# Partial results set aside in SBUF: their 46 additions move from VectorE to GpSimd, and loads are issued between them

## The chip, the core and the metric

One NeuronCore of a Trainium2 chip runs the kernel. The metric is device time in microseconds of one execution; a smaller number is better. The engines are named as the profile names them: PE (TensorE, matmuls), PEld (its weight loads), DVE (VectorE), ACT (ScalarE), POOL (GpSimd) and SP (SyncE, here only a DMA queue). SBUF is the core's working memory, PSUM the banks in which PE accumulates. POOL has two tasks here: it issues the loads (it writes their descriptors) and it can compute on SBUF.

## The reference

```python
# input: (16, 512, 1024) f32, grad_output: (16, 512, 768) f32
grad_weight = np.einsum('bmk,bmn->kn', input, grad_output)   # (1024, 768) f32
```

Batch and m together are 8192 rows. Every element of the result is a sum over all of them, so the result (3 MB) stays on the core while 58.7 MB of input stream past it.

## The kernel before

**Tiling.** The 8192 rows are cut into 32 units of 256 rows; each unit is one load of X (512 KB as bf16) and one of G (384 KB), converted from f32 to bf16 by the DMA on the way in. The result is cut into quarters A, B, C, D (halves of k by halves of n), and each quarter into four row tiles q = 0..3 of 128 x 384. Six units ("s" in LOADS, the first five and the last) are multiplied directly. The other 26 ("P") hold two rows on each partition, so that X and G are 2 x 2 block matrices; these are multiplied with seven block products in place of eight. The products are called A, B, C (which go to the quarters of that name), 1, 5, 6 and 7. The extra operands of products 5, 6 and 7, and the changed ones of B and C, are sums of blocks: three instructions on X (`sum_x`, lines 206, 208, 210) and three on G (`sum_g`, lines 216, 218, 220) for each unit, all on DVE, bf16, with both operands and the result in SBUF. Below they are called **block sums**: 26 x 6 = 156 instructions.

**Sums in SBUF.** `acc` holds the quarters and `macc` the products 1, 5, 6, 7, all f32. There are eight PSUM banks and 32 sums (8 products x 4 tiles), so a sum gets a bank for a few matmuls and is then closed.

**The order** is written out by hand in PLAN, a string of tokens, and each engine executes its own tokens in just that order. Four engines follow the plan: nothing is reordered.

- `B1@4.2`: open tile 1 of product B in bank 4 and do 2 matmuls; `A0.2` goes on in an open bank (`multiply`, matmul on line 328).
- `f`: ACT copies a sum from SBUF into a bank, so that matmuls add to it (`fill`, line 302).
- `c`, `v`: close a bank: ACT copies it to the sum (line 367), or DVE adds it to the sum (line 371; 369 and 364 are its copy and its last step).
- `z...`: the bank is copied to one of 24 slots `aside` (`set_aside`, line 383), so that it comes free at once, and `y...` later adds the slot to the sum (`add_aside`, line 392, DVE, 46 times, f32 128 x 384, both operands in SBUF). 43 of the copies are ACT's, three are DVE's.
- `x`, `g`: a block sum. `w`: merges two sums on POOL near the end (`merge`, line 399, five times).

**Who waits for an addition.** The next writer of that slot, and the next `f`, `c` or `v` of the same sum. Slots are few in use at first (`aside` 0 to 2) and many later.

**Loads.** All are issued on POOL's queue (lines 175 and 176 for units 2 to 31), G before X, in a loop that stands ahead of the plan; nothing stands between them on POOL. Ten pairs of load buffers are held (`PAIRS_HELD`). A load waits until its buffer is free, and, since there are eight semaphores for such loads, until the load eight places before it has landed.

Of the kernel before, what the change touches and what calls it, by code (L numbers as in the profile page):

```python
# [9 lines left out]
P = 128  # L10

LOADS = "sssssPPPPPPPPPPPPPPPPPPPPPPPPPPs"
# [17 lines left out]
    "zcC2.0 D2@6.2 fD3@3 C3@7.2 yC2.0 D0@4.2 zcD2.1 vC3 D3.2 D1@6.2 vD0 cD3 C1@7.2 yD2.1 A3.4 fB3@3 vD1 "  # L30
    "A2.4 vC1 D3@4.2 A1.4 zcD3.0 B1@6.2 yD3.0 B3.2 vB1 C2@4.2 cB3 D0@7.2 vC2 D2@6.2 zcD0.1 C3@3.2 vD2 "
    "fD1@4 C0.2 B0@7.2 zvC3.0 C1@6.2 yD0.1 zcB0.2 B2@3.4 vC1 D1.4 yC3.0 vB2 D0@7.2 cD1 C3@6.2 yB0.2 "
    "zcD0.1 A0.2 g0.5 A0.2 fC2@4 D3@7.2 zvC3.0 C2.2 g1.5 zcD3.2 B1@6.2 yD0.1 cC2 D2@3.2 zvB1.3 B3@7.2 "
    "zcD2.1 B0@4.1 g2.5 B0.1 zcB3.4 C1@6.1 x0.5 C1.2 zcB0.5 A2.3 yC3.0 zcC1.6 10@3.1 x1.5 12@7.1 A1.3 c10 "
    "yD3.2 c12 C2@4.1 x2.5 C3@6.1 C0.1 zcC2.0 g0.6 C0.2 zcC3.2 11@3.1 yB1.3 13@7.1 A3.2 c11 g1.6 A3.1 c13 "
    "50@4.1 yD2.1 51@6.1 52@3.1 c50 A0.1 g2.6 53@7.1 x0.6 c51 A0.1 70@4.1 C0.1 c52 A1.1 v53 71@6.2 c70 "
    "72@3.1 x1.6 72.1 c71 73@7.2 yB3.4 c72 60@4.2 x2.6 61@6.2 c73 g0.7 62@3.2 c60 63@7.2 v61 c62 A2.1 "
    "g1.7 B0@4.2 c63 yC1.6 B2@3.2 zcB0.3 B1@6.1 g2.7 B1.1 A3.1 zcB2.1 yB0.5 13@4.2 zcB1.4 11@7.1 x0.7 "
    "11.1 A2.1 zc13.6 A0.1 v11 C0.1 C1@3.2 x1.7 10@6.2 zcC1.5 yC2.0 B3@4.2 zc10.7 53@7.1 g0.8 53.1 A3.1 "
    "A1.1 zc53.0 x2.7 70@3.2 vB3 51@6.2 zc70.8 C2@7.1 g1.8 C2.1 zc51.9 yC3.2 12@4.2 C3@3.1 zcC2.10 g2.8 "  # L40
    "C3.1 A1.1 x0.8 A0.1 zcC3.2 50@7.2 52@6.3 v12 zc50.11 71@3.1 x1.8 71.1 zc52.12 A2.1 yB0.3 72@4.2 "
    "zc71.13 73@7.1 g0.9 73.1 zc72.3 A3.1 x2.8 61@6.2 zc73.14 g1.9 63@3.2 v61 C0.1 60@4.2 zc63.15 g2.9 "
    "B2@7.2 y13.6 zc60.16 B1@6.2 zcB2.17 10@3.1 x0.9 10.1 A3.1 f62@4 C0.1 vB1 A2.1 zc10.6 50@7.2 x1.9 "
    "62.2 zc50.18 yB2.1 C2@3.2 c62 51@6.1 x2.9 51.1 A1.1 fB0@7 g0.10 A0.1 B3@4.3 vC2 B0.2 zcB3.1 g1.10 "
    "B0.1 12@3.2 v51 cB0 11@4.1 g2.10 11.1 zc12.19 13@6.3 yB1.4 zc11.20 C3@7.1 x0.10 C3.2 C1@3.3 v13 "
    "53@4.1 x1.10 53.2 zcC1.4 70@6.3 vC3 zc53.21 x2.10 52@3.2 zc70.22 g0.11 71@7.2 zc52.23 61@4.2 yC1.5 "
    "A2.1 f62@6 A0.1 g1.11 B2@3.2 v71 62.2 zcB2.5 C0.1 g2.11 A1.1 c62 x0.11 A1.1 A3.2 f73@3 72@7.2 v61 "
    "f60@6 A2.1 73.1 x1.11 73.2 f12@4 v72 60.3 c73 x2.11 12.2 c60 g0.12 63@7.3 c12 y53.0 B1@3.3 f10@6 "
# [3 lines left out]
    "71.3 c70 y10.7 72@4.2 c71 x2.13 72.1 61@7.1 g0.14 f62@3 61.2 A1.1 v72 fB2@6 A2.1 62.2 g1.14 f10@4 "  # L52
    "62.1 v61 B2.3 c62 g2.14 10.2 f11@7 x0.14 10.1 A3.2 cB2 12@3.3 v10 f73@6 x1.14 11.3 v12 73.2 c11 "
    "x2.14 73.1 60@4.1 f63@3 g0.15 60.2 C0.1 c73 y70.8 A0.1 63.2 fB0@7 g1.15 63.1 B1@6.3 v60 c63 B0.1 "
    "g2.15 fC1@4 B0.2 vB1 A1.2 fC2@3 x0.15 A2.2 f13@6 C1.3 vB0 C2.2 cC1 x1.15 C2.1 13.3 y51.9 f50@7 C0.1 "
    "g0.16 cC2 51@4.3 c13 x2.15 50.2 g1.16 f52@3 50.1 v51 53@6.3 c50 g2.16 52.3 fC3@4 v53 A0.2 fB3@7 "
    "x0.16 C3.3 c52 yC2.10 B3.3 f72@6 x1.16 cC3 70@3.3 vB3 72.2 f62@4 g0.17 72.1 f71@7 A3.2 x2.16 62.2 "
    "c72 g1.17 62.1 71.3 v70 fB2@6 C0.1 c62 g2.17 B2.3 v71 f11@4 61@3.1 x0.17 61.2 f12@7 11.3 cB2 v61 "
    "12.2 c11 x1.17 12.1 73@6.3 yC3.2 c12 10@3.1 x2.17 10.2 f60@7 g0.18 63@4.3 v73 60.3 g1.18 fB1@6 A1.2 "
    "v10 A2.2 c60 g2.18 B1.3 v63 A0.2 x0.18 cB1 C0.2 f50@4 C1@3.3 y52.12 A3.1 x1.18 A3.1 50.3 vC1 B0@7.1 "  # L60
    "x2.18 B0.2 c50 g0.19 13@6.3 fC2@3 vB0 A1.1 f53@4 A2.1 C2.1 g1.19 C2.2 v13 53.3 cC2 g2.19 51@7.1 "
    "x0.19 f52@6 51.2 A0.1 c53 A2.1 v51 52.3 f70@3 x1.19 52.1 fC3@4 61@7.3 y50.11 c52 C3.1 g0.20 C3.2 "
    "f72@6 70.1 x2.19 70.2 cC3 g1.20 72.3 v61 c70 C0.1 g2.20 B3@4.4 c72 y71.13 fB2@7 A1.2 y72.3 f71@6 "
    "A3.2 x0.20 B2.3 vB3 12@3.3 cB2 x1.20 71.4 v12 62@7.1 g0.21 62.3 c71 x2.20 f63@3 60@4.2 g1.21 60.1 "
    "f10@6 A0.1 v62 63.3 g2.21 f11@7 10.4 v60 c63 x0.21 11.4 fC1@4 v10 fB1@3 C0.2 c11 A2.1 x1.21 A2.1 "
    "C1.3 y63.15 f73@6 fB0@7 B1.1 x2.21 B1.2 g0.22 cC1 73.4 cB1 y60.16 B0.1 f13@4 g1.22 B0.3 v73 C2@3.2 "
    "cB0 g2.22 C2.1 13.1 x0.22 f51@6 13.3 f53@7 vC2 A1.2 c13 51.1 x1.22 51.3 f50@3 y73.14 53.2 c51 x2.22 "
    "53.2 g0.23 50.4 c53 yB2.17 A0.2 f52@7 g1.23 A3.2 c50 y10.6 70@6.2 g2.23 70.1 f72@3 C3@4.4 y50.18 "
    "x0.23 A2.2 C0.2 v70 72.3 x1.23 f61@6 72.1 52.3 vC3 c72 x2.23 52.1 61.2 g0.24 c52 61.2 y12.19 B3@4.3 "
    "c61 g1.24 B3.1 f12@7 B2@3.4 y11.20 f62@6 g2.24 12.1 x0.24 12.3 62.3 vB2 c12 A1.2 vB3 c62 60@7.2 "  # L70
    "x1.24 f71@3 60.1 A0.1 g0.25 A0.1 fB1@4 A3.2 x2.24 f63@6 71.2 g1.25 71.2 v60 B1.2 c71 g2.25 B1.2 "
    "yB3.1 63.3 f11@3 x0.25 63.1 cB1 C1@7.4 c63 y53.21 11.2 f10@4 x1.25 11.2 f73@6 vC1 10.3 c11 x2.25 "
    "10.1 fC2@7 73.1 g0.26 73.3 c10 yC1.4 C2.2 fB0@3 g1.26 C2.2 c73 y70.22 13@4.3 cC2 g2.26 B0.4 y52.23 "
    "f50@6 x0.26 f53@7 A2.3 cB0 50.4 v13 f51@3 x1.26 53.4 f70@4 v50 51.1 g0.27 51.3 f61@6 x2.26 c53 70.2 "
    "g1.27 70.2 c51 yB2.5 B3@7.2 c70 g2.27 B3.1 61.3 y11.0 f52@3 C0.1 fC3@4 x0.27 C0.3 c61 A1.3 vB3 x1.27 "
    "A0.3 fB2@7 x2.27 C3.2 g0.28 C3.2 52.2 cC3 g1.28 52.2 72@6.1 g2.28 72.3 c52 A3.3 v72 B2.2 x0.28 f62@6 "
    "B2.2 12@4.2 cB2 x1.28 12.2 60@3.1 f71@7 x2.28 60.4 v12 62.1 g0.29 62.4 fB1@4 v60 B1.2 c62 g1.29 B1.2 "
    "f11@3 g2.29 71.4 vB1 63@6.2 c71 x0.29 63.2 11.4 v63 A2.1 x1.29 fC1@6 A2.2 v11 C2@4.3 g0.30 f13@3 "
    "C2.1 10@7.1 x2.29 10.3 vC2 C1.2 g1.30 C1.2 f11@4 v10 13.3 cC1 g2.30 13.1 A1.1 x0.30 A1.2 c13 12@6.2 "
    "f13@3 11.1 x1.30 10@7.1 A0.3 c11 v12 13.1 x2.30 f61@4 C0.3 v10 f62@6 61.4 v13 f60@7 62.2 f63@3 v61 "  # L80
    "60.2 A3.3 v62 f71@4 63.2 v60 f72@6 71.2 v63 f70@7 A0.2 A1.2 v71 f73@3 A2.3 f51@4 wC1 A3.2 73.5 vA3 "
    "vA0 72.3 v73 51.4 vA1 f53@3 wC3 70.4 vA2 53.4 v72 f52@0 v70 fC1@1 C0.2 52.3 v51 fC2@2 f50@6 C1.3 wB1 "
    "fC3@7 vC0 C2.3 fD1@4 v52 C3.5 cC1 wB2 fD2@5 50.4 v53 fB1@1 fD3@0 D2.2 wB3 B1.4 vC2 cC3 fB2@3 v50 "
    "D1.2 cB1 D3.2 B2.5 fD0@2 vD2 fB0@7 vD3 D0.2 fB3@1+6 vB2 B0.7 vD0 vD1 B3.6 vB0 cB3 "
# [8 lines left out]
MERGED = 2  # L93
# [16 lines left out]
def kernel(  # L110
# [6 lines left out]
    nc = tc.nc  # L117
    bf16 = mybir.dt.bfloat16
    f32 = mybir.dt.float32

    B, M, K = input.shape
# [45 lines left out]
    items = []  # L167
    tiles = {}
    for u, kind in enumerate(LOADS):
        pool = pairs if u else head  # L170
        xp = pool.tile([P, 2, K], bf16, name="xp", tag="xp")
        gp = pool.tile([P, 2, N], bf16, name="gp", tag="gp")
        if u >= MERGED:
            rows = slice(2 * u * P, 2 * (u + 1) * P)
            nc.gpsimd.dma_start(out=gp, in_=G[rows, :].rearrange("(p m) n -> p m n", m=2))  # L175
            nc.gpsimd.dma_start(out=xp, in_=X[rows, :].rearrange("(p m) k -> p m k", m=2))  # L176
        for h in range(2):
            s = 2 * u + h
            if s > 0 and u < MERGED:
                nc.gpsimd.dma_start(out=gp[:, h, :], in_=G[s * P : (s + 1) * P, :])  # L180
            if s > 1 and u < MERGED:
                nc.gpsimd.dma_start(out=xp[:, h, :], in_=X[s * P : (s + 1) * P, :])  # L182
            if kind == "s":
                items.append(("s", xp[:, h, :], gp[:, h, :]))
        tiles[u] = (xp, gp)
        if kind == "P":
            items.append(("P", u, None))

# [35 lines left out]
    x0, x1, g0 = items[0][1], items[1][1], items[0][2]  # L226
# [20 lines left out]
    def operands(p, i, q):  # L247
        kind, x, g = items[i]
        k = slice(q * P, (q + 1) * P)
        if kind == "s":  # L250
            half = slice(KH, K) if p in "CD" else slice(0, KH)
            return x[:, half][:, k], g[:, LEFT if p in "AC" else RIGHT]
        u = x
# [134 lines left out]
    def add_aside(p, q, i):  # L388
        laid.remove((p, q, i))
        assert (p, q) not in opened or not opened[p, q][1]  # L390
        dst = sum_of(p, q)
        nc.vector.tensor_add(out=dst, in0=dst, in1=aside[i])  # L392
# [64 lines left out]
```

## Time and profile before

| | |
|---|---|
| device time, median of 3 runs | 162.1 us (162.03 to 162.11) |
| the profiled execution: span, first to last instruction | 160.0 us |
| left outside the span, median less span | 2.1 us |
| PE busy | 155.1 us, 97% |
| DVE busy | 146.8 us, 92% |
| ACT busy | 118.2 us, 74% |
| POOL busy | 39.6 us, 25% |
| the 46 additions on DVE (line 392) | 25.7 us busy |
| the 156 block sums on DVE | 73.1 us busy |
| 60 large loads, from issue to landing | 16.8 us (G), 16.9 us (X) |

The profile is of one execution. "Busy" is the time in which an engine has an instruction in work. Two instructions of DVE or ACT that follow each other overlap a little, so that busy time divided by count is more than the step from one start to the next. A group line of the page gives source line, engine, operation, output and inputs, shape and count; then, behind the bar, busy us and mean ns; then, behind the second bar, how long the engine sat idle just before, and what ended most of that. A digit row cuts the span into 40 slices of 4 us and gives the busy share of each in tenths. The answer by stages cuts the span where it is told to: start and end, length, then busy us and (instruction count) of each engine.

### The profile page before, as it was taken

How to read it: one execution, taken by the hardware profiler on the slowest of the kernel's cores; microseconds unless marked ns; L12 is line 12 of the kernel's file. 1: busy time of each engine (PE TensorE's matmuls, PEld its weight loads, DVE VectorE, ACT ScalarE, POOL GpSimd, SP SyncE). 2: the span in 40 equal slices, each digit the busy share in tenths (PEclk: the TensorE clock that was granted, in tenths of full speed). 3: DMA queues.
4: the chain of work that ended last, by engine and by line, in shares of the span. 5: the costliest groups of instructions: out<-in, count | busy, mean ns of one | idle time of the engine just before them, and what ended most of it. 6: DMA issues, size and time to landing. Idle time of an engine off the chain costs nothing.

```text
span 160.0 us, 3074 instructions
## 1 busy us (share of the span) xinstructions
PE 155.1 (97%) x1057; PEld 98.4 (62%) x1057; DVE 146.8 (92%) x344; ACT 118.2 (74%) x274; POOL 39.6 (25%) x74
## 2 busy tenths in 40 slices
PE   8999899999999999999999999999999999999991
PEld 7666476666666666666656666666666666656661
DVE  0689979999999999999999999999999989998991
ACT  3683444899788788988986596985789855685960
POOL 7442222122221222222122221222222100004510
PEclk9999999999999999999999999999999999999999
DMA  5999999999999999999999999999999999931786
GB/s 174 298 211 215 212 216 213 211 215 212 212 213 213 212 211 213 213 214 214 216 215 213 212 211 214 212 213 210 212 217 212 212 215 215 212 64 45 218 294 234
DMA packets 12447, 33.42 MB, mean 209 GB/s; under 512 B 1424, under 2 KB 4240, under 8 KB 12432
## 3 DMA queue, kind: packets, MB, share of 16 engines
q0 software_dynamic: 9360, 28.64, 90.5%
q1 hardware_dynamic: 2640, 3.41, 6.6%
q10 hardware_dynamic: 432, 1.18, 2.0%
q8 instruction: 8, 0.13, 0.3%
q14 instruction: 7, 0.06, 0.1%
HBM read 58.72 MB, written 3.15 MB: 387 GB/s over the span
## 4 chain that ended last, share of the span: by engine, by line
PE 85%; DMA 8%; POOL 2%; ACT 1%; issue 1%; DVE 1%; ACTq 0%; POOLq 0%
PE bank L328 85%; DMA xp<-in_input_dram 8%; POOL gp L180 1%; POOL xp L182 1%; ACT bank L302 1%; ACT acc L367 1%; DVE acc L369 1%; POOL gp L175 0%; ACT macc L367 0%; ACTq L367 0%; POOLq L441 0%
## 5 line engine op out<-in xcount | busy, mean ns | idle before, releaser
L328 PE MATMUL bank<-gp,xp 128*128 128x384 bf16 (+2 forms) x690 | 109.1, 308 | 0.8 <-DMA xp<-in_input_dram 0.5
L328 PEld LDWEIGHTS <-xp 128*128 128x128 bf16 x690 | 64.6, 98 | 37.9 <-DMA xp<-in_input_dram 0.8
L328 PE MATMUL bank<-ge,xe 128*128 128x384 bf16 x312 | 59.7, 326 | 0.0
L328 PEld LDWEIGHTS <-xe 128*128 128x128 bf16 x312 | 30.3, 98 | 19.0
L302 ACT COPY bank<-macc 128x384 f32<-128x384 f32 x73 | 34.4, 486 | 7.0 <-DVE macc L371 2.5
L367 ACT COPY macc<-bank 128x384 f32<-128x384 f32 x68 | 31.4, 482 | 5.7 <-PE bank L328 5.0
L176 POOL DMA_DIRECT2D xp<-in_input_dram x30 | 15.9, 529 | 53.0 <-DVE ge L218 21.0
L367 ACT COPY acc<-bank 128x384 f32<-128x384 f32 (+1 forms) x39 | 18.3, 477 | 12.3 <-PE bank L328 12.2
L175 POOL DMA_DIRECT2D gp<-in_grad_output_dram x30 | 15.9, 531 | 37.4 <-DMA gp<-in_grad_output_dram 10.4
L371 DVE TENSOR_TENSOR acc<-bank,acc 128x384 f32<-128x384 f32 x45 | 23.7, 555 | 0.6 <-PE bank L328 0.4
L302 ACT COPY bank<-acc 128x384 f32<-128x384 f32 (+2 forms) x45 | 20.9, 480 | 4.3 <-DVE acc L371 1.9
L383 ACT COPY aside<-bank 128x384 f32<-128x384 f32 x43 | 19.1, 483 | 6.0 <-PE bank L328 5.1
L371 DVE TENSOR_TENSOR macc<-bank,macc 128x384 f32<-128x384 f32 x38 | 21.2, 558 | 0.6 <-PE bank L328 0.5
L206 DVE TENSOR_TENSOR xe<-xp 128x1024 bf16<-128x1024 bf16 x26 | 18.0, 692 | 0.0
L392 DVE TENSOR_TENSOR acc<-acc,aside 128x384 f32<-128x384 f32 x26 | 14.5, 556 | 1.3 <-ACT aside L383 1.3
L216 DVE TENSOR_TENSOR ge<-gp 128x768 bf16<-128x768 bf16 x26 | 14.5, 558 | 0.0
L392 DVE TENSOR_TENSOR macc<-macc,aside 128x384 f32<-128x384 f32 x20 | 11.2, 563 | 0.0
L210 DVE TENSOR_TENSOR xp<-xp,xe 128x512 bf16<-128x512 bf16 x26 | 11.0, 425 | 0.1
L208 DVE TENSOR_TENSOR xe<-xe,xp 128x512 bf16<-128x512 bf16 x26 | 11.0, 424 | 0.1
L399 POOL TENSOR_TENSOR acc<-acc,macc 128x384 f32<-128x384 f32 x5 | 5.0, 1000 | 21.6 <-DVE macc L364 19.7
L220 DVE TENSOR_TENSOR gp<-ge,gp 128x384 bf16<-128x384 bf16 x26 | 9.3, 358 | 0.1
L218 DVE TENSOR_TENSOR ge<-gp,ge 128x384 bf16<-128x384 bf16 x26 | 9.3, 359 | 0.0
(20 smaller groups left out, 42.7 us busy)
## 6 DMA issues: line engine op xcount, KB each, us to landing
xp<-in_input_dram POOLq DMA_DIRECT2D x30, 512.0 KB, 16.9
gp<-in_grad_output_dram POOLq DMA_DIRECT2D x30, 384.0 KB, 16.8
out_dram<-acc SPq DMA_DIRECT2D x12, 192.0 KB, 2.0
xf<-in_input_dram ACTq DMA_DIRECT2D x2, 512.0 KB, 5.0
gp<-in_grad_output_dram POOLq DMA_DIRECT2D x3, 192.0 KB, 6.4
out_dram<-acc SPq DMA_DIRECT2D x6, 96.0 KB, 2.2
xp<-in_input_dram POOLq DMA_DIRECT2D x2, 256.0 KB, 7.8
gf<-in_grad_output_dram SPq DMA_DIRECT2D x2, 192.0 KB, 4.4
```

Source lines behind the costliest of these rows:

```text
L175: nc.gpsimd.dma_start(out=gp, in_=G[rows, :].rearrange("(p m) n -> p m n", m=2))
L176: nc.gpsimd.dma_start(out=xp, in_=X[rows, :].rearrange("(p m) k -> p m k", m=2))
L206: nc.vector.tensor_sub(out=xe[:, 0:2, :], in0=x[:, 1::-1, :], in1=x[:, 3::-2, :])
L208: nc.vector.tensor_sub(out=xe[:, 2, :], in0=xe[:, 0, :], in1=x[:, 0, :])
L210: nc.vector.tensor_add(out=x[:, 1, :], in0=x[:, 2, :], in1=xe[:, 2, :])
L216: nc.vector.tensor_add(out=ge[:, 0:2, :], in0=g[:, 0:2, :], in1=g[:, 1::2, :])
L302: nc.scalar.copy(out=tile_[:, t0 : t0 + c1 - c0], in_=sum_of(p, q)[:, c0:c1])
L328: nc.tensor.matmul(tile_[:, t0 : t0 + c1 - c0], stat, mov[:, c0:c1], start=start, stop=True, skip_group_check=True,)
L367: nc.scalar.copy(out=d, in_=b)
L371: nc.vector.tensor_add(out=d, in0=b, in1=d)
L383: copy(out=aside[i], in_=b[:, t0 : t0 + NH])
L392: nc.vector.tensor_add(out=dst, in0=dst, in1=aside[i])
```

## The change

`add_aside` issues its addition on POOL. Since POOL's queue also carries the loads, these can no longer all stand ahead of the plan: the first five units are loaded there as before, and the others are issued by 54 new tokens in the plan, `LG5` (G of unit 5) to `LX31`, each at a place between the additions.

```diff
-    for u, kind in enumerate(LOADS):
...
+    EARLY = 5
...
+    def load(which, u):
+        if u not in tiles:
+            allot(u)
+        rows = slice(2 * u * P, 2 * (u + 1) * P)
+        if which == "G":
+            src, dst = G, tiles[u][1]
+        else:
+            src, dst = X, tiles[u][0]
+        nc.gpsimd.dma_start(out=dst, in_=src[rows, :].rearrange("(p m) n -> p m n", m=2))
+
+    for u in range(EARLY):
+        allot(u)
...
     def add_aside(p, q, i):
...
-        nc.vector.tensor_add(out=dst, in0=dst, in1=aside[i])
+        nc.gpsimd.tensor_add(out=dst, in0=dst, in1=aside[i])
...
     for token in PLAN:
...
+        if op == "L":
+            load(rest[0], int(rest[1:]))
```

The plan is otherwise the same. Its first changed stretch, before and after:

```diff
-    "zcC2.0 D2@6.2 fD3@3 C3@7.2 yC2.0 D0@4.2 zcD2.1 vC3 D3.2 D1@6.2 vD0 cD3 C1@7.2 yD2.1 A3.4 fB3@3 vD1 "
+    "zcC2.0 D2@6.2 fD3@3 C3@7.2 LG5 LX5 LG6 LX6 LG7 yC2.0 D0@4.2 zcD2.1 vC3 D3.2 D1@6.2 vD0 cD3 C1@7.2 "
+    "LX7 yD2.1 A3.4 fB3@3 vD1 A2.4 vC1 D3@4.2 A1.4 zcD3.0 B1@6.2 LG8 yD3.0 B3.2 vB1 C2@4.2 cB3 D0@7.2 vC2 "
```

In the built programs the instructions of PE, ACT and SP are the same in the same order, and DVE's are the same less the 46 additions. POOL's queue has 46 additions more, and between the load `LG7` and the first of them stands the instruction that reloads POOL's program library; before, it stood behind the last load, ahead of the first merge (line 399).

## The prediction

> **What bounds the kernel now.** First the page's busy times and digit rows.
>
> ```profile
> PE 155.1 (97%) x1057; PEld 98.4 (62%) x1057; DVE 146.8 (92%) x344; ACT 118.2 (74%) x274; POOL 39.6 (25%) x74
> ...
> PE   8999899999999999999999999999999999999991
> ...
> DVE  0689979999999999999999999999999989998991
> ...
> POOL 7442222122221222222122221222222100004510
> PEclk9999999999999999999999999999999999999999
> ```
>
> PE is full from the second slice to the last but one, at the full clock: the bound is PE. DVE is nearly as full. Next the groups, for the idle time in front of PE and the price of each operation.
>
> ```profile
> L328 PE MATMUL bank<-gp,xp 128*128 128x384 bf16 (+2 forms) x690 | 109.1, 308 | 0.8 <-DMA xp<-in_input_dram 0.5
> ...
> L371 DVE TENSOR_TENSOR acc<-bank,acc 128x384 f32<-128x384 f32 x45 | 23.7, 555 | 0.6 <-PE bank L328 0.4
> ...
> L206 DVE TENSOR_TENSOR xe<-xp 128x1024 bf16<-128x1024 bf16 x26 | 18.0, 692 | 0.0
> ...
> L392 DVE TENSOR_TENSOR acc<-acc,aside 128x384 f32<-128x384 f32 x26 | 14.5, 556 | 1.3 <-ACT aside L383 1.3
> ...
> L399 POOL TENSOR_TENSOR acc<-acc,macc 128x384 f32<-128x384 f32 x5 | 5.0, 1000 | 21.6 <-DVE macc L364 19.7
> ```
>
> All matmuls on loaded data wait 0.8 us together (those on block sums 0.0), and 0.5 of it is for the first loads, which do not change. So whatever the change frees on DVE, PE can gain some 0.3 us at most: **the change can cost much and win next to nothing.** The question is whether it makes PE wait. For that the stages, with DVE and POOL third and fifth after the length (PE, PEld, DVE, ACT, POOL):
>
> ```profile
> 20.00:36.00 16.00, 16.00 (x116) 10.43 (x114) 14.80 (x34) 11.08 (x27) 3.69 (x7) 1.00 1.07 214
> 36.00:52.00 16.00, 16.00 (x107) 10.04 (x106) 16.00 (x40) 13.79 (x33) 3.91 (x8) 1.00 1.07 213
> ...
> 84.00:100.00 16.00, 16.00 (x109) 10.09 (x108) 16.00 (x41) 11.46 (x27) 3.94 (x8) 1.00 1.07 213
> 100.00:116.00 16.00, 16.00 (x109) 10.07 (x107) 16.00 (x39) 12.89 (x31) 3.97 (x8) 1.00 1.07 212
> ```
>
> From 36 us on DVE has no idle time, yet PE never waits for it: DVE is just fast enough. It feeds PE (block sums) and frees its banks (line 371).
>
> **What the change removes.** DVE's pace is the step between starts:
>
> ```profile
> 26.23 0.55 DVE L392 TENSOR_TENSOR acc<-acc,aside 128x384 f32<-128x384 f32 x1
> 26.69 0.55 DVE L371 TENSOR_TENSOR acc<-bank,acc 128x384 f32<-128x384 f32 x1
> 27.16 0.55 DVE L392 TENSOR_TENSOR acc<-acc,aside 128x384 f32<-128x384 f32 x1
> 27.63 0.55 DVE L371 TENSOR_TENSOR acc<-bank,acc 128x384 f32<-128x384 f32 x1
> 28.09 0.55 DVE L392 TENSOR_TENSOR acc<-acc,aside 128x384 f32<-128x384 f32 x1
> ```
>
> Four steps in 1.86 us, 0.47 each. 46 additions free 46 x 0.47 = 21.6 us of DVE. On PE's path this is worth nothing.
>
> **What it adds on POOL.** By the five merges an addition takes 1.00 us: 46 us. POOL's loads in the same stretch (20 to 128 us, seven stages) are 51 x 0.53 = 27 us, so 73 of 108 us, which fits. The loads are late only by what stands before them: they land 16.8 us after issue and one pair follows another every 4.3 us, so about eight are under way at any time, and an issue that is a few us late leaves the DMA at work. I cost late loads at nothing; the cover is some 15 us.
>
> The additions' own lateness: from 36 us on a slot is written many us ahead of its addition, and POOL's place in the queue is good enough. The first stage is tight. It has 11 additions and 7 loads, 11 x 1.00 + 7 x 0.53 = 14.7 of 16 us, and slots are reused soon. The timeline of ACT writes slot 0 at 19.09, and again at 23.00; DVE added it at 19.61. Following POOL's new order there: load G9 cannot be issued before 27.67 (as before: it waits for an earlier landing), is done at 28.20, and the fifth, sixth and seventh additions come behind it, to 29.2, 30.2 and 31.2. Their slots are next written at 29.03, 29.52 and 30.49 in the trace of before: up to 0.7 us late. ACT idles before several copies there, so this may cost nothing; I take the 0.7 in full, and 0 and 0.7 as its bounds.
>
> **The library reload.** POOL's queue has a reload before its first computing instruction. In before it stood behind the last load:
>
> ```profile
> 125.63 0.53 POOL L176 DMA_DIRECT2D xp<-in_input_dram  x1 [1.89 <-DVE ge L218]
> 144.67 0.99 POOL L399 TENSOR_TENSOR acc<-acc,macc 128x384 f32<-128x384 f32 x1 [18.51 <-DVE macc L364]
> ```
>
> It had 18.5 us of cover. Now it starts at about 19.6, just before the first addition, which must end by 23.00: cover 3.4 - 1.0 = 2.4 us. Its length is not seen: between the 0.04 us of its records and 18.5. A short one is likelier for an instruction with so short a record; I take up to 2.4, which costs nothing, and keep the rest as a rival. The Trainium skill (GPSIMD Engine Reference, Instruction dispatch) gives about 6 us, with no instruction to show for it, for the first call to a freshly loaded library; by that figure 6 - 2.4 = 3.6 us would be added and the sum would be 176.6. No row here shows it.
>
> **VectorE beside GpSimd.** No row of before shows a POOL addition beside a block sum: the merges run beside DVE's lines 359 to 364, which read a PSUM bank and one SBUF operand, and both keep their times (1.00 and 0.55 us). Now both engines will read two SBUF operands each. An addition with two SBUF operands is as quick on DVE (556 ns) as one with one (555), so DVE reads two SBUF streams at once; POOL needs 1.8 times as long for the same addition, as an engine would that fetches its operands in turn. If one of DVE's two ways into SBUF is also POOL's, each must wait for the other. The bounds per addition: 0 (as beside the merges) and a DVE held for the whole 1.00 us. The nearest rows, the merges, say 0, but they lack the second SBUF operand, which is what would collide; so I take exclusion, as a judgement, and work out its price.
>
> DVE starts 288 instructions from 20 to 140 us (the stages' sum), 242 without the additions; 156 are block sums (64%). If POOL gets its way in at the end of a block sum, DVE's next instruction is a block sum with 0.64 and waits 1.00; else it does another for 0.47 and then waits 0.53 with 0.64, else 0.06: 0.64 + 0.36 x (0.34 + 0.02) = 0.77 us. If POOL comes in the middle of another instruction, 0.23 us of it are left: 0.64 x 0.77 + 0.36 x 0.64 x 0.30 = 0.56. Block sums take about six tenths of DVE's remaining time, so 0.6 x 0.77 + 0.4 x 0.56 = 0.69 us held per addition. Against 0.47 freed, DVE loses 0.22 x 46 = 10.1 us. DVE was full, so I put these on PE's path in full. Block sums have some lead that would hide a part (the first, line 216 at 28.6, is used by PE at 34.4), but line 371, in the same queue, frees banks and has none. Bounds: 0, and 46 x (1.00 - 0.47) = 24.4 us.
>
> The Trainium skill (SBUF — State Buffer on-chip working memory, Who interferes with whom) says the same in stronger words: a VectorE instruction with two SBUF inputs contends with a GpSimd instruction that reads SBUF, and the second to issue blocks until the first is done. By that the 10.1 stands; without it the sum is 162.8. No run here has shown it yet.
>
> **The sum.** Profiled execution: span 160.0 + 10.1 + 0.7 = 170.8; with the 2.1 us that lie outside the span, 172.9, against a median of 162.1. I forecast 173.
>
> **Rivals.**
> - *Exclusion as above*: 168 to 181. For it: DVE full, two SBUF operands on both sides. Chance 0.42.
> - *No exclusion, everything hidden*: POOL's 1.00 us fits its windows, the lateness goes into ACT's idle time, PE stays the bound: 162.1, not slower. It decides if the block sums keep their times (692 and 558 ns) beside additions of 1.00 us. For it: the merges, and PE full. Chance 0.15. If besides the freed DVE also removes the 0.3 us of PE's waits: 161.8, chance 0.03.
> - *Little or no exclusion, but POOL late in the first stage*: 0.7 to 0.7 + 3.6 us, for a reload of 6 us, or a milder collision: 162.4 to 168. For it: windows of 3.4 us there. Chance 0.27.
> - *Full price*: DVE held 1.00 us by each addition and a long reload: 162.1 + 24.4 + 3.6 = 190, over 181 in any case. Against it: a third of DVE's remaining work reads a PSUM bank and could go on. Chance 0.13.
>
> **How the numbers follow.** About 0.2% (0.3 us) is what a measurement of this kernel tells from no change. Faster 0.03; within 0.2% 0.15; slower 0.42 + 0.27 + 0.13 = 0.82. A range of 162 to 181 leaves out the full price and the fastest case, 0.16. The likeliest case alone: 168 to 181.
>
> **What would show it.** Right: the means of lines 206 to 220 grow, or gaps open before them, POOL's additions grow over 1.00 us, and PE has idle time released by DVE, most where additions are dense (20 to 52 and 100 to 128 us). Reload: one long POOL gap before the first addition and a PE wait near 23 to 26 us. Wrong: lines 206 to 220 at their old means, DVE at about 76% and PE's idle time still 0.8 us; or the loads late, with the DMA's digit row falling under 9 before slice 35.

## The result, and the profile after

| | time, us (median, lowest to highest) | ratio to the kernel before, 95% interval |
|---|---|---|
| before | 162.06 (161.95 to 162.11) | |
| after | 190.45 (188.52 to 190.91) | 1.173 (1.167 to 1.179) |

The forecast was 173.0, with a range of 162 to 181. The direction was right, and the two engines do exclude each other as the prediction took it; but the change cost 28.4 us where 10.8 were forecast, and two terms of the sum failed.

The page of the kernel after: busy times, and the digit rows of 40 slices, now 4.7 us each (the span is 188.8 us).

```profile
PE 163.2 (86%) x1057; PEld 98.7 (52%) x1057; DVE 163.4 (87%) x298; ACT 119.4 (63%) x274; POOL 88.6 (47%) x120
...
PE   8898998817969699999978989993999299999992
...
DVE  0799577997698999999999998999799976997992
...
POOL 7432679996450930462480325789167600002440
PEclk9999999985899999999999999997899969999999
DMA  5999999999999999999999994999986930000487
```

DVE has 46 instructions less and is busy 16.6 us *longer* (146.8 before). PE's row has holes, the deepest in slices 9, 28 and 32, and at or just behind all three PEclk falls: the waits also cost TensorE its clock. The DMA row, 9 from slice 2 to slice 35 before, has its first hole in slice 25.

Groups of the page (behind the first bar: busy us, mean ns; behind the second: idle before, and what ended most of it):

```profile
L346 PE MATMUL bank<-gp,xp 128*128 128x384 bf16 (+2 forms) x690 | 111.8, 309 | 16.2 <-DVE gp L238 9.2
...
L410 POOL TENSOR_TENSOR acc<-acc,aside 128x384 f32<-128x384 f32 x26 | 27.5, 1067 | 24.7 <-DVE acc L389 13.8
...
L389 DVE TENSOR_TENSOR acc<-bank,acc 128x384 f32<-128x384 f32 x45 | 23.4, 552 | 6.8 <-PE bank L346 6.5
...
L224 DVE TENSOR_TENSOR xe<-xp 128x1024 bf16<-128x1024 bf16 x26 | 21.7, 836 | 0.0
...
L236 DVE TENSOR_TENSOR ge<-gp,ge 128x384 bf16<-128x384 bf16 x26 | 17.9, 690 | 0.3
```

The block sums are longer: line 224 took 692 ns before (as line 206), and line 236 took 359, as the page of before has it:

```profile
L218 DVE TENSOR_TENSOR ge<-gp,ge 128x384 bf16<-128x384 bf16 x26 | 9.3, 359 | 0.0
```

Line 389, which reads a PSUM bank and one SBUF operand, is as before (555). PE now waits for block sums (line 238 is one), and DVE for PE's banks. The stages, in the columns of before:

```profile
20.00:36.00 16.00, 14.45 (x100) 8.99 (x99) 11.91 (x17) 8.74 (x20) 13.59 (x16) 1.00 1.08 214
36.00:52.00 16.00, 10.88 (x56) 5.89 (x55) 13.21 (x16) 8.03 (x20) 11.60 (x16) 0.79 1.07 213
...
100.00:116.00 16.00, 15.27 (x102) 9.23 (x100) 14.85 (x32) 11.12 (x25) 4.73 (x7) 1.00 0.87 168
```

From 36 to 52 us DVE starts 16 instructions where it started 40 (8 of the 40 were additions), and is busy 13.2 us with them.

**Held time** is from here on what the stretched block sums (and, where they run on DVE, the additions with two SBUF operands) last beyond their mean in the kernel before, summed over the single records. In the kernel after 38 of the 156 block sums are stretched, by 34.0 us. A sum held for over 1 us is called a **long hold**; an addition itself takes 1.0 to 1.1 us. On PE's side, 28.5 of the 28.8 us that the span grew are accounted for: waits of 24.8 us (1.1 before), and 5.2 us lost by matmuls at the low clock (0.4 before). A wait of PE is counted here from one start to the next, less what a matmul's step takes; so it is up to 0.16 us longer than the idle time that a view shows.

### The profile page after: what moved, and what is told of

Read it like the earlier page. It is cut to its first block, busy times and chain, and to the rows that moved or that the text cites. A ratio compares the mean times of both kernels' runs of the same rounds, so it can differ in the third digit from the quotient of the medians.

```text
span 188.8 us, 3094 instructions
## 1 busy us (share of the span) xinstructions
PE 163.2 (86%) x1057; PEld 98.7 (52%) x1057; DVE 163.4 (87%) x298; ACT 119.4 (63%) x274; POOL 88.6 (47%) x120
## 4 chain that ended last, share of the span: by engine, by line
PE 47%; DVE 29%; DMA 10%; POOL 6%; issue 4%; ACT 1%; POOLq 0%; DVEq 0%; ACTq 0%
PE bank L346 47%; DMA gp<-in_grad_output_dram 7%; DVE xp L228 5%; DVE ge L234 4%; DVE ge L236 4%; DVE gp L238 4%; DVE xe L226 3%; POOL acc L410 3%; DVE xe L224 3%; DMA xp<-in_input_dram 3%; DVE acc L389 2%; DVE macc L389 2%; DVE macc L387 1%; POOL gp L201 1%; POOL gp L189 1%
## 5 line engine op out<-in xcount | busy, mean ns | idle before, releaser
L346 PE MATMUL bank<-gp,xp 128*128 128x384 bf16 (+2 forms) x690 | 111.8, 309 | 16.2 <-DVE gp L238 9.2
L346 PE MATMUL bank<-ge,xe 128*128 128x384 bf16 x312 | 65.0, 343 | 5.3 <-DVE xe L224 4.3
L320 ACT COPY bank<-macc 128x384 f32<-128x384 f32 x73 | 34.4, 486 | 17.8 <-DVE macc L389 10.8
L385 ACT COPY macc<-bank 128x384 f32<-128x384 f32 x68 | 31.7, 484 | 15.1 <-PE bank L346 14.3
L410 POOL TENSOR_TENSOR acc<-acc,aside 128x384 f32<-128x384 f32 x26 | 27.5, 1067 | 24.7 <-DVE acc L389 13.8
L410 POOL TENSOR_TENSOR macc<-macc,aside 128x384 f32<-128x384 f32 x20 | 21.6, 1083 | 26.6 <-ACT macc L385 25.8
L401 ACT COPY aside<-bank 128x384 f32<-128x384 f32 x43 | 19.2, 483 | 12.7 <-PE bank L346 10.4
L385 ACT COPY acc<-bank 128x384 f32<-128x384 f32 (+1 forms) x39 | 18.3, 477 | 13.3 <-PE bank L346 13.1
L320 ACT COPY bank<-acc 128x384 f32<-128x384 f32 (+2 forms) x45 | 20.8, 479 | 3.7 <-DVE macc L389 1.7
L224 DVE TENSOR_TENSOR xe<-xp 128x1024 bf16<-128x1024 bf16 x26 | 21.7, 836 | 0.0
L234 DVE TENSOR_TENSOR ge<-gp 128x768 bf16<-128x768 bf16 x26 | 20.0, 769 | 0.0
L189 POOL DMA_DIRECT2D gp<-in_grad_output_dram x30 | 16.6, 555 | 7.0 <-DMA gp<-in_grad_output_dram 5.7
L236 DVE TENSOR_TENSOR ge<-gp,ge 128x384 bf16<-128x384 bf16 x26 | 17.9, 690 | 0.3
L228 DVE TENSOR_TENSOR xp<-xp,xe 128x512 bf16<-128x512 bf16 x26 | 16.8, 648 | 0.3
L238 DVE TENSOR_TENSOR gp<-ge,gp 128x384 bf16<-128x384 bf16 x26 | 15.0, 578 | 0.3
L226 DVE TENSOR_TENSOR xe<-xe,xp 128x512 bf16<-128x512 bf16 x26 | 14.7, 566 | 0.2
## 6 DMA issues: line engine op xcount, KB each, us to landing
gp<-in_grad_output_dram POOLq DMA_DIRECT2D x30, 384.0 KB, 12.2
```

Source lines behind the costliest of these rows:

```text
L189: nc.gpsimd.dma_start(out=dst, in_=src[rows, :].rearrange("(p m) n -> p m n", m=2))
L224: nc.vector.tensor_sub(out=xe[:, 0:2, :], in0=x[:, 1::-1, :], in1=x[:, 3::-2, :])
L226: nc.vector.tensor_sub(out=xe[:, 2, :], in0=xe[:, 0, :], in1=x[:, 0, :])
L228: nc.vector.tensor_add(out=x[:, 1, :], in0=x[:, 2, :], in1=xe[:, 2, :])
L234: nc.vector.tensor_add(out=ge[:, 0:2, :], in0=g[:, 0:2, :], in1=g[:, 1::2, :])
L236: nc.vector.tensor_add(out=ge[:, 2, :], in0=g[:, 3, :], in1=ge[:, 0, :])
```

## The experiments

| kernel | us | ratio (95%) | held, us | of it in long holds |
|---|---|---|---|---|
| e1_loads_only | 161.8 | 1.000 (0.999 to 1.001) | 0 | 0 |
| e2_no_adds | 161.7 | 0.998 (0.997 to 0.999) | 0 | 0 |
| e3_write_only | 162.0 | 1.000 (0.999 to 1.001) | 0 | 0 |
| e4_extra_adds | 189.9 | 1.173 (1.169 to 1.178) | 28.7 | 9.7 |
| e5_extra_copies | 170.8 | 1.057 (1.053 to 1.061) | 8.5 | 0 |
| e8_extra_fenced | 179.5 | 1.108 (1.105 to 1.111) | 17.1 | 0 |
| e11_extra_23 | 174.5 | 1.077 (1.076 to 1.079) | 13.3 | 1.0 |
| e10_extra_no_real | 175.8 | 1.086 (1.084 to 1.087) | 26.2 | 7.7 |
| e6_first_22 | 175.6 | 1.085 (1.080 to 1.089) | 15.3 | 10.1 |
| e7_last_24 | 177.2 | 1.094 (1.090 to 1.098) | 20.8 | 10.1 |
| e9_adds_first | 193.2 | 1.193 (1.190 to 1.196) | 36.7 | 21.7 |
| after | 190.4 | 1.173 (1.167 to 1.179) | 34.0 | 17.3 |
| e14_loads_earlier | 188.8 | 1.166 (1.163 to 1.169) | 33.9 | 19.0 |
| e12_loads_early | 184.8 | 1.142 (1.140 to 1.144) | 32.2 | 13.7 |
| e17_fence_adds | 183.9 | 1.136 (1.127 to 1.144) | 33.1 | 12.3 |
| e15_early_fenced | 176.4 | 1.093 (1.087 to 1.099) | 23.0 | 0 |
| e13_fenced | 173.0 | 1.067 (1.065 to 1.069) | 24.2 | 0 |
| e16_fence_loads | 172.9 | 1.066 (1.065 to 1.068) | 23.9 | 0 |

### The parts alone: e1, e2, e3

Each edits `add_aside` of the kernel after; the loads stay with the tokens.

```diff
-        nc.gpsimd.tensor_add(out=dst, in0=dst, in1=aside[i])
+        nc.vector.tensor_add(out=dst, in0=dst, in1=aside[i])     # e1
+                                                                 # e2: nothing
+        nc.gpsimd.memset(aside[i], 0.0)                          # e3
+        nc.gpsimd.memset(dst, 0.0)                               # e3
```

> The second half of the change alone: the loads are issued by tokens between the other steps, but the 46 additions stay on VectorE. Theory X (a GpSimd addition and a block sum exclude each other in time, and that holds VectorE): 162.1 us, as before, since nothing but loads stands in GpSimd's queue until the merges. Theory Q (the place of the loads in the queue is what costs): above 165.

> The 46 additions are left out altogether (so the sums lack the set-aside parts); loads by tokens. This shows what VectorE's freed 21.6 us are worth on TensorE's path. Both theories: 161.8 to 162.1, TensorE is the bound; VectorE's idle time grows by about 21 us.

> Each addition is replaced by two GpSimd memsets, one of the slot and one of the sum (so the sums lose what they held): GpSimd waits for the same producers, and the next users wait for GpSimd, but it reads no SBUF. Theory X, if the collision is in reading: block sums keep 692 and 558 ns, 162 to 164 us. Theory Q (GpSimd waits in order for closes, the loads behind it come late): stays above 180 us with block sums at their old durations too. If writing collides as well, block sums stretch and the time is 175 to 190.

Measured: 161.8, 161.7 and 162.0. The loads in their new places cost nothing. The 46 additions on DVE cost 0.3 us at most: PE is the bound. And in e3, GpSimd waits for the same slots, writes slot and sum, and is waited for as with the additions, and nothing moved. Its groups of POOL and DVE:

```profile
L410 POOL MEMSET aside<- 128x384 f32 x46 | 20.1, 437 | 0.0
...
L224 DVE TENSOR_TENSOR xe<-xp 128x1024 bf16<-128x1024 bf16 x26 | 17.8, 684 | 0.4 <-DMA xp<-in_input_dram 0.4
```

Block sums beside GpSimd's writes keep their time. The waits that the change moves to POOL are harmless as long as POOL is through quickly; the two writes take 0.87 us, an addition 1.07.

### The collision alone: e4, e5, e8

The real additions are back on DVE, and GpSimd does 46 instructions on spare tiles that wait for nothing and that nobody waits for.

```diff
+        nc.vector.tensor_add(out=dst, in0=dst, in1=aside[i])
+        nc.gpsimd.tensor_add(out=spare[1], in0=spare[0], in1=spare[0])   # e4
+        nc.gpsimd.tensor_copy(out=spare[1], in_=spare[0])                # e5, in its place
+        nc.gpsimd.memset(spare[0][:, 0:1], 0.0)                          # e8, ahead of e4's
```

> The 46 real additions stay on VectorE, and at their places GpSimd does 46 extra ones of the same size on spare tiles, which nobody waits for and which wait for nobody. Theory X: each holds VectorE some 0.7 us and nothing is freed in return, so 162.1 + 46 x 0.7 = 194 us, less if block sums' lead hides some: 180 to 200. Theory Q: no waits, so 162.1 us.

> As the run with 46 extra additions on GpSimd (real ones on VectorE, extra ones on spare tiles), but each extra one is a copy, which reads one operand from SBUF and not two. If any reading by GpSimd excludes a block sum: sums are stretched again, by about the length of a copy each time (shorter than an addition, some 0.5 us), and the time lies between 165 and 180. If only two operands on GpSimd's side collide: 162, block sums at 692 and 558 ns.

> As the run with 46 extra additions (189.9 us), but before each stands a one-column memset on GpSimd that the addition waits for, so that an addition behind a load issue is not begun before that issue is over. Theory: a sum is held from the moment at which GpSimd takes up an addition behind a load issue, before the addition's own record starts (in the 189.9 us run 4.4 of 19.1 us held lay in load issues). Then the part in load issues falls to about 0 and the time to 180 to 186. Rival, the held time in load issues comes from the issues themselves: it stays at 4 us or more, and the time stays at 190 or above.

Measured: e4 189.9, about as slow as the kernel after though none of GpSimd's work is needed. So the collision alone, without a wait for GpSimd's results, can cost that much. (e4 is not the kernel after without its waits: DVE has the 21.6 us of additions still to do, and e4's extra additions, which read one tile twice, take 0.84 us in the median where the real ones take 1.01.) The Trainium skill (SBUF — State Buffer, Who interferes with whom) says that a VectorE instruction with two SBUF inputs contends with a GpSimd instruction that reads SBUF, and not with one that only writes; e3 (0 us held) and e4 (28.7 us) agree. e5 shows that one operand is enough:

```profile
L414 POOL COPY spare<-spare 128x384 f32<-128x384 f32 x46 | 46.4, 1008 | 0.7
```

The copies hold DVE for 8.5 us in all. Their mean of 1008 ns is not the price of a copy: 19 of the 46 take 0.51 to 0.52 us, and nine take over 1 us, because here DVE holds GpSimd. The longest, and the instruction of DVE that ends it:

```profile
114.66 4.16 POOL L414 COPY spare<-spare 128x384 f32<-128x384 f32 x1
```

```profile
118.36 0.55 DVE L392 TENSOR_TENSOR macc<-bank,macc 128x384 f32<-128x384 f32 x1
```

From 114.21 to 118.36 DVE issues only block sums and additions, which have two SBUF operands, one directly behind the other and each in its normal time. Line 392 is the first that reads a PSUM bank, and the copy ends 0.45 us after its start. All nine copies of over 1 us end 0.43 to 0.45 us after the start of such an instruction. So the exclusion works both ways: in these nine GpSimd got no turn between two instructions of DVE with two SBUF operands that followed each other without a gap.

In e8 the write of one column takes 113 ns and the addition waits for it. The time falls by 10.4 us, to just under the 180 to 186 that were expected. In e4, 5.8 us of the held time lie in load issues of GpSimd, in e8 none. In these kernels nothing was freed on DVE, and the extra time is the held time: 27.9 us for 28.7 (e4), 8.9 for 8.5 (e5), 17.6 for 17.1 (e8), and 12.5 for 13.3 (e11, below).

### How much, and what the freed time is worth: e11, e10, e6, e7

```diff
+        added.append(i)
+        if len(added) % 2:                                               # e11: e4 with every other one
+            nc.gpsimd.tensor_add(out=spare[1], in0=spare[0], in1=spare[0])
-        nc.vector.tensor_add(out=dst, in0=dst, in1=aside[i])             # e10: e4 without DVE's
+        engine = nc.gpsimd if len(added) < 22 else nc.vector             # e6; e7 has >= 22
+        engine.tensor_add(out=dst, in0=dst, in1=aside[i])
```

> As the run with 46 extra additions, but only at every second place, 23 of them; the 46 real ones stay on VectorE. If the time grows by just the time that VectorE is held: some half of 28 us, 172 to 179, and within 1.5 us of 162 plus the held time in its own trace. If there is a slack that hides the first part: under 170.

> As the run with 46 extra additions on spare tiles (189.9 us), but the 46 real ones are left out (the sums lack the set-aside parts): VectorE gets its 21.6 us back while GpSimd collides as before, and nobody waits for GpSimd. If freed time counts in full, as the forecast took it: 189.9 - 21.6 = 168. If it counts for a quarter, as the held times of the runs so far say: 182 to 186.

> Only the first 22 additions (up to 62 us) are on GpSimd, the other 24 on VectorE as before. Held time decides: in the changed kernel 13.0 of 34.0 us of held block sums and 9 us of TensorE's waiting lie before 62 us, so 170 to 175 us. By the forecast's net price of 0.22 us each it would be 162.1 + 22 x 0.22 = 167.

> Only the last 24 additions (from 64 us) are on GpSimd. Held time decides: 21.0 of 34.0 us of held block sums lie there, so 175 to 182 us, and with the run of the first 22 the extra times add up to about 28. By the net price of 0.22 us each: 162.1 + 24 x 0.22 = 167.

Measured: 174.5, 175.8, 175.6 and 177.2. e11 and e7 are as expected, e6 is 0.6 us above its range, and both halves are far from the 167 of the forecast's net price. e10 fell between its two expectations, and so refutes both: against e4, DVE has the additions' 21.6 us less to do, and 14.1 us come back. The freed time is worth something where DVE is held, but not its full length. e10 also has as little work on DVE as the kernel after, and is 14.6 us faster; in the kernel after the additions also wait for slots and sums, and are waited for. These waits do not cost that by themselves, since e16 below has them all and takes 172.9; but the holds differ. In e4 and e10, too, additions stand behind load issues, and no hold is over 1.27 us. The two halves (13.5 and 15.1 us over 162.1) add up to the 28.4 of the whole: the cost is spread over both halves.

### Where the loads stand: e9, e12, e14

The `L` tokens are moved: in e9 each behind the next addition, in e12 those of units 14 to 31 ahead of one addition more, in e14 of two. The first places of each kind:

```diff
-    ... LG5 LX5 LG6 LX6 LG7 yC2.0 ...  LG14 yB2.1 LX14 yB1.4 ...
+    ... yC2.0 LG5 LX5 LG6 LX6 LG7 ...                            # e9
+    ... LG14 y13.6 LX14 yB2.1 LG15 yB1.4 ...                     # e12
+    ... LG14 LX14 y13.6 LG15 yB2.1 ...                           # e14
```

> The changed kernel with its loads moved one place: each load token stands behind the next addition and not in front of it, so that fewer additions are ready while a load issue before them is still running. Theory: less of the held time lies in load issues (6.2 of 34.0 us in the changed kernel), so 184 to 188 us. Rival, loads issued still later make the data late: 191 or more.

> The changed kernel with the 36 large loads from unit 14 on issued one addition earlier in GpSimd's queue; nothing else differs. Theory: the time of the changed kernel (190.4 us) is the price of VectorE held behind GpSimd's reads and of TensorE's low clock after its long waits; the late load seen near 148 us is a small part of it, and an addition that stands behind one more load is still held during that load's issue. Then the time stays at 188 to 192, the held time at 32 to 37 us. Rival: the loads that come late, because they stand in the queue behind additions that wait for their slots, cost the unexplained part: then the late landing at 148 us and the wait of 3.7 us behind it go, with the low clock after it, and the time falls to 184 to 187 with the held time as before.

> The changed kernel with the large loads from unit 14 on issued two additions earlier in GpSimd's queue (e12: one). Theory: e12 left the DMA with one to three loads under way after 107 us, so loads are still late there, and the time falls further, to 181 to 184. Rival: what late loads cost is gone with e12, and the rest is the held time, which stays at 32: 184 to 186.

Measured: 193.2, 184.8 and 188.8. e9 went the wrong way, with more held in load issues (8.0 us), not less. Its time and e12's were those of the rivals, that late loads cost several us; e14, with its loads earlier still, is 4 us slower than e12 and outside both of its ranges. The traces settle it: in e9, e12, e14 and the kernel after, each load from unit 7 to unit 30 has landed at least 9.3 us before DVE starts its first block sum on it. No load is late there, so the rivals do not stand; that two of them had the right time was luck. The three times have the order of the last column of the table: 13.7, 19.0 and 21.7 us in long holds. The kernel after does not fit in (17.3 us, but slower than e14).

### The holds behind load issues: e13, e16, e17, e15

A one-column write ahead of the addition, which the addition waits for: at all additions (e13), at the 34 directly behind a load (e16), at the other 12 (e17), and at all in the kernel e12 (e15).

```diff
+        nc.gpsimd.memset(aside[i][:, 0:1], 0.0)                          # e13, e15
+        if behind[-1] == "load":                                         # e16; e17 has "add"
+            nc.gpsimd.memset(aside[i][:, 0:1], 0.0)
         nc.gpsimd.tensor_add(out=dst, in0=dst, in1=aside[i])
```

> The changed kernel with a one-column write ahead of each addition, which the addition waits for, so that GpSimd cannot take up an addition's reads while a load issue ahead of it is still running. The write zeroes the first of the 384 columns of the slot, so this column's share of the set-aside results is left out. Theory: of the 34.0 us held in the changed kernel 6.2 lie in load issues; these go, and the time falls by about as much, to 182 to 186. Rival: VectorE is held there where it would have waited anyway, or the late loads set the pace there: the held time falls and the time stays at 188 to 191.

> The changed kernel with the one-column write (that column's share of the slot is left out, as in e13) only ahead of additions that stand directly behind a load in GpSimd's queue. Theory: what costs is that VectorE is held from the moment GpSimd has taken up the addition, while the load issue ahead of it still runs; then nearly all of e13's gain is here: 172 to 177, 24 to 27 us held, none in load issues. Rival: what costs are pairs of additions with no gap, through which VectorE stays held: 184 to 190.

> The changed kernel with the one-column write only ahead of additions that stand directly behind another addition. Theory: the load issues ahead of the other additions still hold VectorE: 186 to 191, some 6 us held in load issues. Rival: the gap between additions is what frees VectorE: 173 to 182.

> e12 and e13 together: loads from unit 14 on one addition earlier, and the one-column write ahead of each addition (which leaves out one column of 384 of the set-aside results). Theory: the two prices are different waits and add up: 190.4 less 5.6 less what e13 wins, some 177 to 181, with 26 us held. Rival: they are the same wait seen twice, and the time is that of the better of the two, 182 to 185.

Measured: 173.0, 172.9, 183.9 and 176.4. More work on POOL makes the kernel 17.5 us faster, and the write ahead of the 34 additions behind a load gives all of it (e16, as expected). The same write ahead of the other 12 gives 6.6 us (e17), in neither of its two ranges. e15 is just under its 177 to 181. e13 expected 182 to 186 and was far off: the held time falls by 9.8 us, more than the 6.2 that lie in load issues, and the kernel's time by 17.5. The timeline of the kernel after, POOL first, then DVE (start, length, line, operation):

```profile
38.81 0.57 POOL L189 DMA_DIRECT2D gp<-in_grad_output_dram  x1
39.38 0.54 POOL L189 DMA_DIRECT2D xp<-in_input_dram  x1
39.92 1.95 POOL L410 TENSOR_TENSOR acc<-acc,aside 128x384 f32<-128x384 f32 x2
```

```profile
39.31 3.25 DVE L236 TENSOR_TENSOR ge<-gp,ge 128x384 bf16<-128x384 bf16 x1
42.59 1.03 DVE L238 TENSOR_TENSOR gp<-ge,gp 128x384 bf16<-128x384 bf16 x1
```

The sum on line 236 takes 0.36 us alone and would have ended at 39.67, ahead of the additions. It is held for 2.89 us: 0.61 while the load issues before them still run, 1.95 through both additions, and 0.33 into the load issue behind them. This last part is not rare: of the 6.2 us held in load issues, 2.6 lie ahead of an addition that the same sum is held by, and 3.3 behind one. PE pays for it:

```profile
43.68 0.80 PE L346 MATMUL bank<-gp,xp 128*128 128x384 bf16 x3 [5.12 <-DVE gp L238]
```

The same place in e16, POOL and then DVE (its line 238 is the kernel after's 236):

```profile
39.52 0.57 POOL L191 DMA_DIRECT2D gp<-in_grad_output_dram  x1
40.08 0.54 POOL L191 DMA_DIRECT2D xp<-in_input_dram  x1
40.60 0.12 POOL L413 MEMSET aside<- 128x1 f32 x1
40.81 2.17 POOL L415 TENSOR_TENSOR acc<-acc,aside 128x384 f32<-128x384 f32 x2
```

```profile
39.78 0.55 DVE L236 TENSOR_TENSOR ge<-gp 128x768 bf16<-128x768 bf16 x1
...
40.71 0.34 DVE L238 TENSOR_TENSOR ge<-gp,ge 128x384 bf16<-128x384 bf16 x1
41.09 1.04 DVE L240 TENSOR_TENSOR gp<-ge,gp 128x384 bf16<-128x384 bf16 x1
```

The first sum runs beside the load issues in its normal time, and the second beside the write and the start of the addition; the third, which falls into the first of two additions, is held 0.68 us and gets its turn at the hand-over to the second. No hold in e16 or e13 exceeds 0.83 us. In the kernel after ten do, over 1 us each, 17.3 us together. The page of e16 shows what that is worth to PE:

```profile
PE   8798999989899899999999989998979799999992
...
PEclk9999999999999999999999999999999999999999
```

PE's waits fall from 24.8 to 12.2 us, the longest from 5.28 to 1.10, and the clock stays full (0.5 us at the low clock for 5.2). 12.6 + 4.7 is 17.3 of the 17.6 us between the spans. e17 shows the other side: with the write at the other 12 additions 12.3 us of long holds remain, and the time is 183.9. A write that the addition does not wait for was not tried; so it is not shown whether the wait or the gap of some 0.2 us between load issue and addition ends the long holds.

Kernels with all additions on GpSimd and long holds thus take longer than e16: with 12.3, 13.7, 19.0, 17.3 and 21.7 us in long holds (e17, e12, e14, after, e9) it is 11.0, 11.9, 15.9, 17.5 and 20.3 us. Without any, e13 takes 0.1 us and e15 3.5 us longer than e16. This is a correlation, and not a strict one; the step from after to e16 alone takes the long holds away by a direct edit.

e15 is 3.4 us slower than e13, with as little held. Its longest wait of PE, 3.29 us of idle time, is for a bank that ACT empties late, and ACT had waited for an addition:

```profile
67.31 0.53 POOL L186 DMA_DIRECT2D gp<-in_grad_output_dram  x1 [1.57 <-DMA gp<-in_grad_output_dram]
68.03 0.99 POOL L408 TENSOR_TENSOR macc<-macc,aside 128x384 f32<-128x384 f32 x1
```

```profile
69.04 0.48 ACT L398 COPY aside<-bank 128x384 f32<-128x384 f32 x1 [3.96 <-POOL macc L408]
```

The load, placed ahead of the addition, cannot be issued until the load eight places before it has landed, at 66.78; the addition behind it comes late, then ACT's copy into the slot, and then the copy that empties PE's bank. So here a load that is placed earlier pushes an addition back.

## Why the prediction was wrong, point by point

- **PE is the bound, and freeing DVE wins at most 0.3 us: right.** e2 wins 0.3.
- **The loads cost nothing: right,** for their new places (e1) and for the time at which they come. The sign that the prediction named for late loads did show: the DMA row falls under 9 in slice 25, and from 114 us on one to four loads are under way where eight were forecast. But none is late: from unit 7 on each has landed at least 9.3 us before its first block sum. (The chain of waits names a load at 143.92 to 148.67 us ahead of line 224. That sum is of unit 26, whose X landed at 127.0; the load is unit 30's and only uses the same semaphore. What held DVE there was line 236, for 2.76 us, and then line 238, for 0.83.)
- **POOL late by 0.7 us in the first stage: not shown as a cost.** In the kernel after ACT does wait for GpSimd's additions, 1.5 us in all and 1.0 at most (at 30.67). In e3 GpSimd waits for the same slots and costs nothing; whether any of the 1.5 us reached PE was not separated.
- **The library reload in 2.4 us of cover: right.** In the kernel after the first addition starts 0.1 us behind the load before it:

```profile
19.47 0.53 POOL L189 DMA_DIRECT2D gp<-in_grad_output_dram  x1 [1.35 <-DMA gp<-in_grad_output_dram]
20.10 1.01 POOL L410 TENSOR_TENSOR acc<-acc,aside 128x384 f32<-128x384 f32 x1
```

  The 6 us of the Trainium skill (GPSIMD Engine Reference, Instruction dispatch) are not to be seen here.
- **Exclusion, instruction against instruction: right.** 31 of the 38 stretched sums of the kernel after end as if they had begun 0.13 to 0.14 us before the end of an addition; in e8 all 41 do (0.14 to 0.15 us). The other seven get their turn in a load issue behind an addition, 0.3 to 1.0 us after its end.
- **"0.69 us held per addition": the step that failed,** though its number looks right: 34.0/46 is 0.74. The prediction took it that DVE is held only while an addition runs ("a DVE held for the whole 1.00 us" was its upper bound for one), and summed short holds. That is how e16 behaves, with 23.9/46 = 0.52. In the kernel after, nine of the ten long holds lie in part in a load issue ahead of or behind an addition, and two of these nine span two additions besides. The ten make half of the held time.
- **"Against 0.47 freed ... on PE's path in full": the term that failed by most.** The prediction itself says that the 21.6 us freed are worth nothing on PE's path; then it credits them in full against the held time. By the same sum the kernel after has 34.0 us held and costs 28.4, so that only 5.6 of the 21.6 us came back. Against the forecast that is 2.3 us more held (34.0 for 31.7) and 16.0 us less credited. The rest became idle time of DVE, which waits for PE's banks (6.8 us ahead of line 389 on `acc`, 0.6 before). In e16 the 23.9 us held cost 10.8, so 13.1 were credited; e10 gave back 14.1. That e16 costs just the 10.8 us that were forecast is luck: two errors of about the same size cancel, 23.9 - 13.1 for 31.7 - 21.6.
- **TensorE's clock was not in the forecast.** 4.7 us more at the low clock than in e16.

The forecast fell short by 17.4 us. The step from the kernel after to e16 shows that 17.5 us hang on the additions directly behind load issues, as 12.6 us of PE's waits and 4.7 us of its clock: long holds, which a mean price per addition does not show, stop PE for up to 5.28 us at a time, and DVE's freed time did not make up for it. That the two numbers are alike is due to the coincidence in e16. The rival "full price" (190) had the time nearly right by luck: the mean hold was 0.74 us and not 1.00, and no reload is seen.

**Left open:** why an addition waiting behind a load issue already keeps VectorE out, why the hold can last into the load issue behind it, and why holds of over 1.27 us show only where the additions also wait for slots and sums. That GpSimd takes the addition up while it still issues the load fits the timelines, but no run looks inside it. The Trainium skill (GPSIMD Engine Reference, Instruction dispatch) states that each of GpSimd's cores begins the next instruction once its own share of the present one is finished, and (When to use GPSIMD) that a pair of the cores does a DMA's descriptors; the others could then begin the addition while that pair is still at the load. No run here shows it.

No kernel with additions on GpSimd is as fast as the one before; the best has 172.9, and it leaves out one column of 384 of the set-aside results. With the additions left out altogether it is 161.7, so there was nothing to win.

## What to carry to other kernels

Price an instruction that is moved from VectorE to GpSimd by what it does to VectorE's other instructions with two SBUF operands, not by whether GpSimd has the time: here each addition freed 0.47 us and held VectorE for 0.74. Where GpSimd must read SBUF beside a busy VectorE, keep its reading instructions away from its load issues, or put a short write that they wait for in between: that was worth 17.5 us here (the write used here zeroes a column that is needed; a correct kernel with one was not built). And a mean price per instruction says little when a few holds are long, since one wait of TensorE of several us costs the wait and then the clock.

## What the hardware showed that was not expected

- A load issue alone stretches no sum (in the kernel before, the sums on lines 218 and 220 never took over 0.37 us), and an addition with the write ahead of it held for 0.83 us at most. Load issues and additions in a row held for up to 2.89 us, and in e14, with four additions in the row, for 4.32.
- One write of 113 ns that the addition waits for ends the long holds.
- GpSimd is held as well: a copy of 0.52 us took up to 4.16 us while VectorE went through instructions with two SBUF operands without a gap, and ended 0.45 us after the start of the first that read a PSUM bank.
- The copy of 128 x 384 f32 takes GpSimd 0.51 to 0.52 us where nothing holds it, the addition 1.00, and the write alone 0.44.
- At waits of 5.28, 3.09 and 3.71 us the granted clock of TensorE fell to 0.5 in the kernel after, for 6.8, 3.4 and 3.4 us, and at one of 2.30 us in e8, for 3.4; at one of 3.46 us in e15 and one of 3.08 us in e7 it did not. The Trainium skill (TensorE: Matmul & The Clock Gate, Part 1: The HAM clock gate) has the clock fall after an idle window of about 3.4 us and rise after a busy one as long: the lengths agree, while the wait that it takes was here anything from 2.30 us to over 3.46.
